# A PEER mixer's second products: weights of four experts per load, first products loaded into the lower parts' buffers, routing recorded between the steps of the weights' making

## Chip, cores and metric

The kernel runs on one core of one Trainium2 chip. The metric is the device time of one execution in microseconds, 3498.06 us before the change (median of three runs, 3488.26 to 3505.14).

## What is computed

A decoder block of 1024 tokens and width 1024: two attention mixers, memory attention, and then a PEER mixer. In the PEER mixer each token has, for each of 8 heads, the 16 best of 128 x 128 experts; an expert is one row of `u` and one row of `v`:

```python
q = (hf @ w_q).reshape(n, PEER_HEADS, 2, PEER_HALF)
sc = einsum('nhcd,hckd->nhck', q, sub_keys)
s_top, i_top = top_k(sc, PEER_TOPK)
...
best_s, pos = top_k(cand_s, PEER_TOPK)
best_i = take_along_axis(cand_i, pos)
g = softmax(best_s)
...
a = einsum('cd,ced->ce', hc, u[ic])
a = gelu(a, approximate=False) * gc
out = einsum('ce,ced->cd', a, v[ic])
```

## The kernel before

Tokens are cut into eight blocks of 128. The attention phases and all products that feed the mixer end about 1629 us after the start of the span; the change leaves their work alone. Blocks 0 to 3 get their mixer by gathers: GpSimd (POOL) fetches 128 rows of `u` (L1035) or of `v` (L1051) by an indirect DMA, and VectorE (DVE) takes a product with them (L1038 for `u`, L1057 for `v`). There are 1024 such gathers, 512 KB each. They are a lane of a pacer (`pace`), which records one of them after each so many microseconds of TensorE work, and run beside everything else, to the end.

Blocks 4 to 7 get theirs in `dense` (L1190), by full products over all 16384 experts in 128 parts of 128; below, "expert" stands for such a part. For each expert there is a first product, `first` (24 matmuls into `acc`: tokens of the four blocks against 128 rows of `u`, L135 to L137), a Gelu, a product with the expert's weights `wl` (L1252, which are zero where a token did not choose it), and a second product with 128 rows of `v`. Every operand is split into two parts that TensorE multiplies at full rate: ACT copies it to the upper part (L112), DVE subtracts to the lower (L113), and three matmuls stand for one. So `uraw` becomes `uT0` and `uT1`, `vraw` becomes `v0` and `v1`, the weighted Gelu becomes `c0` and `c1`.

In time `dense` has these stages.

- Weights stage, 1630 to 2209 us. `weights` (L1116) makes the table of weights for the four blocks as a lane of the pacer, beside the first products of the first 48 experts (`early`), whose Gelu goes to DRAM as `ga` (256 KB each). For each block it first runs the routing (`route`, top 16 and the choice of 16 among the sums, nearly all on DVE, 21 pieces), then two transposes and the codes (L1131 to L1152), then 32 steps: two matmuls to `dot` (L1164), a Relu on ACT (`oh`, L1168), a comparison on DVE (`ah`, L1170), four matmuls to `out` (L1174), a copy on ACT to `wbuf` (L1176). After 16 steps a half of the block is stored to `Wd` by eight stores of 512 KB (L1184) on SP's queue, released one at a time in the pieces of the routing and the steps that follow. What of this lane is left when the 48 first products are recorded is drained without any beside it.
- Start of the second products, 2209 to 2244 us.
- Stage of the loaded first products (the "ga stage" below), 2244 to 2561 us: groups 0 to 10 of second products. A group is four experts: `second` loads their `vraw` (512 KB each, four buffers), splits them and issues 96 matmuls, into four PSUM tiles that are kept over all groups (`kept`) and into two that DVE adds to `accu` (L1281). For the next group, `group` loads the weights of two experts at a time (`wl`, 128x8x128, L1244), and for each expert its stored first product (`c`, one buffer, L1248).
- Steady stage, 2561 to 3478 us: groups 11 to 31, where `group` makes the first products itself, so that a group has 96 first and 96 second matmuls. Then the end, to 3497 us.

SP issues all of these loads in one order, and waits in it: an issue that waits for a buffer holds up all behind it. The order on each engine is set by a scheduler at build time.

## Time and profile before

| | us |
|---|---|
| median of three runs | 3498.06 |
| the profiled execution | 3498.35 |
| its span | 3496.6 |
| TensorE busy (matmul) | 3027.1 |
| DVE busy | 2851.4 |
| ACT busy | 1399.1 |
| POOL busy | 1402.9 |

Busy times are sums over the whole span, and no engine of them is the limit all the way; so the stages are read apart, each with its busy times, the granted clock of TensorE and the share of time that the DMA engines were busy, and then the waits of each engine inside a stage.

### The profile page before, as it was taken

Reading aid. Unit: us, or ns where it says so; the run is one execution under the profiler, and the core shown is the slowest. Engines: PE = TensorE matmul, PEld = TensorE weight load, DVE = VectorE, ACT = ScalarE, POOL = GpSimd, SP = SyncE. Lnnn points to the kernel's source line nnn. Section 1 sums busy time; section 2 is a strip of 40 time slices with the busy share of each in tenths; the row PEclk is TensorE's granted clock in tenths of the full one; section 3 lists DMA queues with packets and bytes.
Section 4 is the critical chain, followed back from the end, with each engine's and each line's share of the span. In section 5 each row is a group of like instructions: output and inputs, shape, how many; then the busy total and the mean of one; then the engine's idle time right before and its main releaser. Section 6 shows DMA issues by size and latency. Waiting matters only on the chain. (4 is left out here: it accounts for less than half of the span.)

```text
span 3496.6 us, 42268 instructions
## 1 busy us (share of the span) xinstructions
PE 3027.1 (87%) x13234; PEld 2292.2 (66%) x13234; DVE 2851.4 (82%) x6623; ACT 1399.1 (40%) x2537; POOL 1402.9 (40%) x1122
## 2 busy tenths in 40 slices
PE   8999888798788798777998896587899999999997
PEld 6778766553345675445676674466677888787886
DVE  6656554588968989887999888687799999899998
ACT  5756344245656441323546465222122222222222
POOL 0010000012245346653122665424457666776665
PEclk9999999899898899888999998799899999999999
DMA  4575443335789579887485999989899999999998
GB/s 139 163 187 136 168 136 137 128 121 187 215 285 303 145 263 359 305 322 281 141 294 210 372 366 345 381 305 326 304 349 373 384 381 371 359 365 384 377 380 285
DMA packets 394210, 964.64 MB, mean 276 GB/s; under 512 B 36713, under 2 KB 146049, under 8 KB 392577
## 3 DMA queue, kind: packets, MB, share of 16 engines
q0 software_dynamic: 155264, 560.01, 45.1%
q1 hardware_dynamic: 238720, 401.94, 33.5%
q8 instruction: 104, 1.70, 0.2%
q14 instruction: 122, 0.99, 0.1%
HBM read 871.64 MB, written 90.18 MB: 275 GB/s over the span
## 5 line engine op out<-in xcount | busy, mean ns | idle before, releaser
L1035 POOL DMA_INDIRECT rows<-in_peer_u_dram,ii x512 | 689.0, 1346 | 916.8 <-DVE rows L1038 365.5
L1051 POOL DMA_INDIRECT rows<-in_peer_v_dram,ii x512 | 649.6, 1269 | 425.4 <-DVE h3s L1057 290.3
L1057 DVE SCALAR_TENSOR_TENSOR h3s<-rows,wexp,h3s 128x1024 f32<-128x1024 f32 x508 | 651.0, 1282 | 36.3 <-DMA rows<-in_peer_v_dram,ii 27.4
L1038 DVE SCALAR_TENSOR_TENSOR rows<-rows,h3s 128x1024 f32<-128x1024 f32 x512 | 611.6, 1219 | 79.1 <-DMA rows<-in_peer_u_dram,ii 75.7
L135 PE MATMUL acc<-fT,uT 128*128 128x512 f32 x1024 | 415.1, 405 | 43.3 <-ACT uT L112 23.9
L137 PE MATMUL acc<-fT,uT 128*128 128x512 f32 x1024 | 412.3, 403 | 13.8 <-DVE uT L113 13.7
L136 PE MATMUL acc<-fT,uT 128*128 128x512 f32 x1024 | 409.6, 400 | 0.0
L112 ACT ACTIVATE c<-wl 128x512 fp32r<-128x512 f32 x128 | 80.1, 631 | 812.2 <-PE out L136 461.6
L149 POOL TENSOR_TENSOR rstd<-msq,mhalf 128x1 f32<-128x1 f32 (+1 forms) x42 | 35.3, 840 | 592.9 <-DVE msq L147 582.5
L135 PEld LDWEIGHTS acc<-fT,uT 128*128 128x128 f32 x1024 | 196.8, 192 | 88.7 <-ACT uT L112 24.8
L137 PEld LDWEIGHTS acc<-fT,uT 128*128 128x128 f32 x1024 | 196.7, 192 | 66.5 <-DVE uT L113 20.9
L136 PE MATMUL kept<-v,c 128*128 128x512 f32 x512 | 206.7, 406 | 34.5 <-DVE v L113 34.5
L135 PE MATMUL kept<-v,c 128*128 128x512 f32 x512 | 202.3, 401 | 37.8 <-ACT v L112 36.9
L112 ACT ACTIVATE uT<-uraw 128x1024 fp32r<-128x1024 f32 x128 | 135.5, 1059 | 246.8 <-PE acc L136 130.5
L136 PEld LDWEIGHTS acc<-fT,uT 128*128 128x128 f32 x1024 | 196.9, 192 | 38.7
L113 DVE TENSOR_TENSOR w<-wraw,w 128x512 fp32r<-128x512 f32 (+1 forms) x176 | 116.8, 680 | 118.6 <-ACT w L112 112.0
L135 PE MATMUL out<-v,c 128*128 128x512 f32 x512 | 204.1, 399 | 8.9 <-DVE accu L1281 8.9
L137 PE MATMUL kept<-v,c 128*128 128x512 f32 x512 | 203.9, 398 | 0.0
L136 PE MATMUL out<-v,c 128*128 128x512 f32 x512 | 202.9, 396 | 0.0
L137 PE MATMUL out<-v,c 128*128 128x512 f32 x512 | 202.6, 396 | 0.0
L568 ACT ACTIVATE junk<-W,xb 128x384 bf16<-128x384 f32 (+5 forms) x186 | 163.7, 880 | 75.7 <-DVE xb L566 55.2
L112 ACT ACTIVATE w<-wraw 128x512 fp32r<-128x512 f32 (+1 forms) x176 | 105.9, 619 | 186.5 <-PE acc L136 81.8
(361 smaller groups left out, 6780.8 us busy)
## 6 DMA issues: line engine op xcount, KB each, us to landing
uraw<-in_peer_ut_dram SPq DMA_DIRECT2D x128, 512.0 KB
vraw<-in_peer_v_dram SPq DMA_DIRECT2D x128, 512.0 KB
Wd<-wbuf SPq DMA_DIRECT2D x64, 512.0 KB
wl<-Wd SPq DMA_DIRECT2D x64, 512.0 KB
wraw<-in_w_in_dram SPq DMA_DIRECT2D x40, 512.0 KB
fraw<-in_w_in_dram SPq DMA_DIRECT2D x32, 512.0 KB
wraw<-in_w_out_dram SPq DMA_DIRECT2D x24, 512.0 KB
ga<-gelu SPq DMA_DIRECT2D x48, 256.0 KB
```

Source lines behind the costliest of these rows:

```text
L112: self.nc.scalar.activation(hi, src, AF.Copy)
L113: self.last_dve = self.nc.vector.tensor_tensor(lo, src, hi.bitcast(F32), op=OP.subtract).ins
L135: nc.tensor.matmul(out, l[0], r[0], start=start, stop=False)
L136: nc.tensor.matmul(out, l[0], r[1], start=False, stop=False)
L137: self.last_pe = nc.tensor.matmul(out, l[1], r[0], start=False, stop=stop).ins
L149: nc.gpsimd.tensor_tensor(r, v, self.mhalf[:, :n], op=OP.pow)
L568: nc.scalar.activation(junk[:, :(b + 1) * P], self.W[b], AF.Sign, bias=xb[:, j:j + 1].bitcast(F32), accum_out=s[:, j:j + 1])
L1035: nc.gpsimd.indirect_dma_start(out=u, out_offset=None, in_=a["peer_u"][0], in_offset=bass.IndirectOffsetOnAxis(ap=ii[:, j:j + 1], axis=0))
L1038: nc.vector.scalar_tensor_tensor(u, u, 1.0, h3, op0=OP.mult, op1=OP.mult, accum_out=aa[:, j:j + 1])
L1051: nc.gpsimd.indirect_dma_start(out=v, out_offset=None, in_=a["peer_v"][0], in_offset=bass.IndirectOffsetOnAxis(ap=r["ii"][:, j:j + 1], axi ...
L1057: nc.vector.scalar_tensor_tensor(o, v, w[:, j:j + 1], o, op0=OP.mult, op1=OP.add)
```

## The change

Four things are changed. The load of weights brings those of four experts, a whole group (128x8x256, 1 MB, in runs of 1 KB), in place of two (512 KB, in runs of 512 bytes), still into two buffers: 32 loads for 64. The stored first product has no tile of its own any more: it is loaded into the expert's `c1`, which has seven buffers, and which the split overwrites later. `vraw` has three buffers for four. In `weights` the routing of block j+1 is recorded in the steps of block j, one piece in each of the first 21 steps, and a piece no longer releases a store. On the side, the Gelu of the gathered rows is made in place (`wexp` goes) and `aa` has two buffers for three. The line numbers of the code behind L1120 are higher by up to four in the kernel after.

```diff
@@ -1029,7 +1029,7 @@
         ii = r["ii"]
         h3 = ep.tile([P, D], F32, name="h3s", bufs=1)
         nc.sync.dma_start(h3, self.h3[b])
-        aa = r["aa"] = ep.tile([P, P], F32, name="aa", bufs=3)
+        aa = r["aa"] = ep.tile([P, P], F32, name="aa", bufs=2)
         for j in range(P):
             u = self.rows()
             nc.gpsimd.indirect_dma_start(out=u, out_offset=None, in_=a["peer_u"][0],
@@ -1041,8 +1041,8 @@
     def gathered_v(self, b, r):
 
         nc, a, ep = self.nc, self.a, self.ep
-        w = ep.tile([P, P], F32, name="wexp", bufs=1)
-        nc.scalar.activation(w, r["aa"], AF.Gelu)
+        w = r["aa"]
+        nc.scalar.activation(w, w, AF.Gelu)
         nc.vector.tensor_tensor(w, w, r["gg"], op=OP.mult)
         o = ep.tile([P, D], F32, name="h3s", bufs=1)
         for j in range(P):
@@ -1121,12 +1121,12 @@
         wb = self.wb
         self.make_codes()
         stores = []
+
+        r = {}
+        yield from self.route(blks[0], r)
         for j, b in enumerate(blks):
-            r = {}
-            for us in self.route(b, r):
-                if stores:
-                    stores.pop(0)()
-                yield us
+            rn = {}
+            ahead = self.route(blks[j + 1], rn) if j + 1 < len(blks) else iter(())
             t = self.ps.tile([P, 512], F32, name="out", bufs=2)
             nc.tensor.transpose(t[:, :P], r["ids"].rearrange("p h s -> p (h s)"), self.ident)
             nc.tensor.transpose(t[:, P:2 * P], r["g"].rearrange("p h s -> p (h s)"), self.ident)
@@ -1176,13 +1176,15 @@
                 nc.scalar.activation(wbuf[:, :, m:m + 4].rearrange("p e n -> p n e"), o, AF.Copy)
                 if stores:
                     stores.pop(0)()
-                yield 1.0
+                yield 1.0 + next(ahead, 0.0)
                 if m + 4 == H:
                     for e0 in range(0, P, 16):
                         def store(e0=e0, at=2 * j + n0 // H, wbuf=wbuf):
                             with self.tc.issue_after(self.last_load):
                                 nc.sync.dma_start(self.Wd[at, :, e0:e0 + 16], wbuf[:, e0:e0 + 16])
                         stores.append(store)
+            yield from ahead
+            r = rn
         while stores:
             stores.pop(0)()
             yield 3.0
@@ -1239,18 +1241,19 @@
             def group(gi):
                 cs = []
                 for e in range(gi * G, gi * G + G):
-                    if e % 2 == 0:
-                        w2 = sp.tile([P, 2 * ND, 2, P // 2], F32, name="wl", bufs=2)
-                        nc.sync.dma_start(w2, self.Wd[:, :, e:e + 2].rearrange("j p e n -> p j e n"))
-                    w = w2[:, :, e % 2]
+                    if e % G == 0:
+                        wg = sp.tile([P, 2 * ND, G, P // 2], F32, name="wl", bufs=2)
+                        nc.sync.dma_start(wg, self.Wd[:, :, e:e + G].rearrange("j p e n -> p j e n"))
+                    w = wg[:, :, e % G]
+                    ch = [sp.tile([P, DT], F32R, name=f"c{j}", bufs=7) for j in range(2)]
                     if e in ga:
-                        c = sp.tile([P, DT], F32, name="c", bufs=1)
+
+                        c = ch[1].bitcast(F32)
                         nc.sync.dma_start(c, ga[e])
                     else:
                         c = first(e)
                         nc.scalar.activation(c, c, AF.Gelu)
                     nc.vector.tensor_tensor(w, c.rearrange("p (j n) -> p j n", j=2 * ND), w, op=OP.mult)
-                    ch = [sp.tile([P, DT], F32R, name=f"c{j}", bufs=7) for j in range(2)]
                     self.split(w, *[x.rearrange("p (j n) -> p j n", j=2 * ND) for x in ch])
                     cs.append(ch)
                 return cs
@@ -1391,7 +1394,7 @@
 WHOLE = {("P", 1), ("G", 1), ("M", 1)}
 PAIRS = {(2, 0)}
 KEEP, A_BUFS, O_BUFS = 4, 2, 2
-U_BUFS, V_BUFS = 3, (4, 4, 4)
+U_BUFS, V_BUFS = 3, (4, 4, 3)
 SELECT_EACH = (5.0, 7.0)
 U_EACH, ROUTE_EACH = (1.9, 1.8, 1.9, 1.3, 2.0), 3.0
 ROUTE_LAG, EXPERT_LAG = 300, 3000
```

Three places show what this moves. The first is SP's queue at the start of the second products; a name like `c_18903<-ga_13694` is the load of one stored first product. Before:

```order
L1244 DMA wl<-Wd 128x8x128 [waits DMAHW2_49,PE_49]
L1248 DMA c<-ga_13695 128x512 [waits DMAHW3_49]
L1244 DMA wl<-Wd 128x8x128 [waits DMAHW4_49]
L1263 DMA vraw<-in_peer_v_dram 128x1024 [waits DMAHW5_49,PE_49]
L1263 DMA vraw<-in_peer_v_dram 128x1024 [waits DMAHW6_49]
L1248 DMA c<-ga_13780 128x512 [waits DMAHW7_49,DMAHW3_49,DVE_49]
L1263 DMA vraw<-in_peer_v_dram 128x1024 [waits DMAHW0_49]
L1263 DMA vraw<-in_peer_v_dram 128x1024 [waits DMAHW1_49,Pool_49]
L1248 DMA c<-ga_13853 128x512 [waits DMAHW7_49,DMAHW2_49,DVE_49]
L1263 DMA vraw<-in_peer_v_dram 128x1024 [waits DMAHW5_49,Activation_49]
```

And with the change:

```order
L1246 DMA wl<-Wd 128x8x256 [waits DMAHW2_49,PE_49]
L1252 DMA c_18903<-ga_13694 128x512 [waits DMAHW3_49]
L1252 DMA c_18909<-ga_13779 128x512 [waits DMAHW6_49,DMAHW7_49,DMAHW5_49,DMAHW4_49]
L1252 DMA c_18915<-ga_13852 128x512
L1252 DMA c_18921<-ga_13953 128x512
L1246 DMA wl<-Wd 128x8x256
L1252 DMA c_18929<-ga_14054 128x512 [waits DMAHW0_49]
L1252 DMA c_18935<-ga_14112 128x512 [waits DMAHW1_49]
L1252 DMA c_18941<-ga_14165 128x512 [waits DMAHW2_49]
L1266 DMA vraw<-in_peer_v_dram 128x1024 [waits DMAHW3_49]
L1266 DMA vraw<-in_peer_v_dram 128x1024 [waits DMAHW4_49]
L1266 DMA vraw<-in_peer_v_dram 128x1024 [waits DMAHW5_49]
```

Seven loads of first products and two of weights stand ahead of the first `vraw`, for one and two before; the names read `c_...` although the tile is `c1`.

The second is DVE at the boundary of two groups in the ga stage (`v1` is the lower part of an expert's `v`, the rows L1252 or L1256 the product of a stored first product with its weights, L1281 or L1284 the addition to `accu`, L1038 a gather's product). Before:

```order
L113 TENSOR_TENSOR c1_20316<-wl_20303,c0_20315 128x512
L113 TENSOR_TENSOR v1_20510<-vraw_20511,v0_20509 128x1024
L1281 TENSOR_TENSOR accu_18901<-accu_18901,out_20460 128x512
L113 TENSOR_TENSOR c1_20483<-wl_20477,c0_20482 128x512
L113 TENSOR_TENSOR c1_20490<-wl_20477,c0_20489 128x512
L113 TENSOR_TENSOR v1_20516<-vraw_20517,v0_20515 128x1024
L1252 TENSOR_TENSOR wl_20493<-c_20495,wl_20493 128x8x64
L113 TENSOR_TENSOR v1_20522<-vraw_20523,v0_20521 128x1024
L113 TENSOR_TENSOR c1_20499<-wl_20493,c0_20498 128x512
L113 TENSOR_TENSOR v1_20528<-vraw_20529,v0_20527 128x1024
L1252 TENSOR_TENSOR wl_20493<-c_20502,wl_20493 128x8x64
```

And with the change:

```order
L113 TENSOR_TENSOR v1_20448<-vraw_20449,v0_20447 128x1024
L1256 TENSOR_TENSOR wl_20237<-c1_20258,wl_20237 128x8x64
L1284 TENSOR_TENSOR accu_18899<-accu_18899,out_20404 128x512
L1256 TENSOR_TENSOR wl_20421<-c1_20424,wl_20421 128x8x64
L113 TENSOR_TENSOR c1_20258<-wl_20237,c0_20257 128x512
L1256 TENSOR_TENSOR wl_20421<-c1_20430,wl_20421 128x8x64
L113 TENSOR_TENSOR c1_20424<-wl_20421,c0_20423 128x512
L1256 TENSOR_TENSOR wl_20421<-c1_20436,wl_20421 128x8x64
L113 TENSOR_TENSOR c1_20430<-wl_20421,c0_20429 128x512
L113 TENSOR_TENSOR v1_20454<-vraw_20455,v0_20453 128x1024
L113 TENSOR_TENSOR c1_20436<-wl_20421,c0_20435 128x512
L113 TENSOR_TENSOR v1_20460<-vraw_20461,v0_20459 128x1024
```

Between the first and the second `v1` of a group stand four products with loaded first products, for none before (there one stands between the second and the third). On SP the four loads that these products need stand together, and wait for TensorE; without the change each waits for DVE alone:

```order
L1252 DMA c_19516<-ga_15418 128x512 [waits DMAHW2_49,PE_49]
L1252 DMA c_19685<-ga_15549 128x512 [waits PE_49]
L1252 DMA c_19691<-ga_15653 128x512 [waits DMAHW4_49,PE_49]
L1252 DMA c_19697<-ga_15761 128x512 [waits DMAHW5_49,PE_49]
L1266 DMA vraw<-in_peer_v_dram 128x1024 [waits DMAHW6_49,DVE_49]
L1266 DMA vraw<-in_peer_v_dram 128x1024 [waits DMAHW7_49,DVE_49]
L1246 DMA wl<-Wd 128x8x256 [waits DMAHW0_49,DVE_49]
```

The third is TensorE behind the last matmul of the 48 early first products. Before:

```order
L136 MATMUL acc<-fT_12994,uT_18248 128x512
L137 MATMUL acc<-fT_12993,uT_18249 128x512
L1131 MATMUL out<-ident,ids 128x128
L1132 MATMUL out<-ident,gw 128x128
L1151 MATMUL out<-ident,bi 112x128 x8
L1164 LDWEIGHTS code_18387
L1164 MATMUL dot<-codes,code_18387 128x512
L1151 MATMUL out<-ident,bi 112x128 x8
L1164 LDWEIGHTS code_18409
```

And with the change:

```order
L136 MATMUL acc<-fT_12993,uT_18124 128x512
L137 MATMUL acc<-fT_12992,uT_18125 128x512
L1164 LDWEIGHTS code_17101
L1164 MATMUL dot<-codes,code_17101 128x512
L1164 LDWEIGHTS code_17123
L1164 MATMUL dot<-codes,code_17123 128x512
L1164 LDWEIGHTS code_17101
L1164 MATMUL dot<-codes,code_17101 128x512
L1164 LDWEIGHTS code_17123
L1164 MATMUL dot<-codes,code_17123 128x512
L1174 MATMUL out<-ah,oh 128x128 x3
```

Before, the transposes and codes of the last block come next, and then its 32 steps. With the change it is the steps of the block before the last: 45 steps are left without first products beside them.

## Rows read from the trace of the kernel before

**Rows 1.** the page, busy time of each engine over the span.

```profile
PE 3027.1 (87%) x13234; PEld 2292.2 (66%) x13234; DVE 2851.4 (82%) x6623; ACT 1399.1 (40%) x2537; POOL 1402.9 (40%) x1122
```

**Rows 2.** five stages: stretch, length, busy us of each engine, granted clock, DMA share, GB/s.

```profile
1630.00:2209.00 579.00, 493.61 (x2551) 386.34 (x2552) 510.32 (x1535) 308.01 (x390) 224.13 (x180) 0.94 0.79 288
2209.00:2244.00 35.00, 0.90 (x4) 0.48 (x3) 15.49 (x15) 3.64 (x5) 11.06 (x11) 0.57 1.04 399
2244.00:2561.00 317.00, 269.80 (x1054) 211.85 (x1054) 249.49 (x343) 72.92 (x98) 122.72 (x96) 0.90 0.91 313
2561.00:3478.00 917.00, 895.11 (x3892) 734.06 (x3890) 870.32 (x1049) 252.15 (x330) 614.07 (x446) 0.99 1.00 371
3478.00:3497.00 19.00, 0.07 (x1) 0.00 (x0) 13.16 (x15) 3.45 (x6) 3.44 (x3) 0.55 0.46 170
```

**Rows 3.** the same for two stretches late in the weights stage.

```profile
2110.00:2140.00 30.00, 10.55 (x40) 7.71 (x41) 21.57 (x34) 7.95 (x12) 15.12 (x11) 0.54 0.94 351
...
2170.00:2200.00 30.00, 22.61 (x147) 17.90 (x145) 27.65 (x31) 24.59 (x30) 20.24 (x16) 1.00 1.02 408
```

**Rows 4.** DVE's waits, 1629 to 2216 us: total us, times, longest us.

```profile
DVE rows L1038 <- DMA rows<-in_peer_u_dram,ii: 21.4, 14, 4.9
...
DVE v L935 <- DMA so<-pq: 5.5, 3, 3.2
```

**Rows 5.** TensorE's waits in the same window.

```profile
PE out L1151 <- DVE bi L1146: 31.9, 6, 17.4
```

**Rows 6.** timeline of SP's queue from 2195 us: start, length, instruction.

```profile
2216.88 1.35 SPq L1244 DMA_DIRECT2D wl<-Wd  x1
2218.28 4.82 SPq L1248 DMA_DIRECT2D c<-ga  x1
2223.15 1.73 SPq L1244 DMA_DIRECT2D wl<-Wd  x1
2224.98 11.06 SPq L1263 DMA_DIRECT2D vraw<-in_peer_v_dram  x2
```

**Rows 7.** timeline around the first second product; in brackets the idle time ahead.

```profile
2239.43 0.69 DVE L1252 TENSOR_TENSOR wl<-c,wl 128x512 f32<-128x512 f32 x1 [10.06 <-DMA c<-ga]
...
2243.64 0.79 PE L135 MATMUL kept<-v,c 128*128 128x512 f32 x1 [34.10 <-ACT v L112]
```

**Rows 8.** DVE's waits, 2244 to 2561 us.

```profile
DVE wl L1252 <- DMA c<-ga: 33.3, 24, 2.9
DVE wl L1252 <- DMA wl<-Wd: 17.9, 5, 5.0
DVE wl L1252 <- issue: 6.8, 2, 3.6
```

**Rows 9.** TensorE's waits, 2209 to 2561 us.

```profile
PE kept L135 <- ACT v L112: 36.9, 2, 34.1
PE kept L136 <- DVE v L113: 34.5, 18, 4.7
```

**Rows 10.** DVE's lines, 2244 to 2561 us: busy us, mean ns of one, idle before.

```profile
L113 DVE TENSOR_TENSOR v<-vraw,v 128x1024 fp32r<-128x1024 f32 x44 | 53.1, 1218 | 0.5 <-ACT v L112 0.5
L1057 DVE SCALAR_TENSOR_TENSOR h3s<-rows,wexp,h3s 128x1024 f32<-128x1024 f32 x32 | 41.0, 1280 | 0.2
L1252 DVE TENSOR_TENSOR wl<-c,wl 128x512 f32<-128x512 f32 x47 | 32.5, 691 | 58.2 <-DMA c<-ga 33.3 <-DMA wl<-Wd 17.9 <-issue 6.8
...
L1281 DVE TENSOR_TENSOR accu<-accu,out 128x512 f32<-128x512 f32 x39 | 26.6, 682 | 6.5 <-PE out L137 6.4
```

**Rows 11.** timeline of SP's queue in the ga stage.

```profile
2424.58 0.32 SPq L1248 DMA_DIRECT2D c<-ga  x1
```

**Rows 12.** timeline of DVE in the ga stage.

```profile
2428.81 0.69 DVE L1252 TENSOR_TENSOR wl<-c,wl 128x512 f32<-128x512 f32 x1 [1.38 <-DMA c<-ga]
```

**Rows 13.** a stretch of 100 us in the steady stage.

```profile
2760.00:2860.00 100.00, 100.00 (x443) 82.80 (x442) 98.97 (x95) 25.30 (x33) 67.74 (x52) 1.00 1.01 379
```

**Rows 14.** TensorE's waits, 2561 to 3478 us.

```profile
PE acc L135 <- DVE wl L1252: 19.3, 10, 4.8
```

## Prediction, made before the kernel with the change was run

> **What bounds the kernel now.** I read the busy times of the whole span first [rows 1]: TensorE 87%, DVE 82%. No engine is full throughout, so one limit can't be named for all of it. I read the stages next [rows 2], and there three cases are to be seen. In the weights stage DVE works 510.32 of 579 us and TensorE 493.61: DVE is nearer to its limit. In the ga stage, 317 us, TensorE works 269.80, DVE 249.49, and the DMA engines have a share of 0.91: nobody is full, so it is waits that decide. In the steady stage TensorE works 895.11 of 917, DVE 870.32, DMA 1.00: everything is full. Between the first two lie 35 us in which TensorE does nearly nothing. What the change can return is therefore at most the idle time of TensorE in each stage: 85, 34, 47 and 22 us.
>
> Then the waits. In the ga stage TensorE waits for the lower part of `v` from DVE, 34.5 us in 18 waits, and 34.1 us once at the start [rows 9]. DVE in turn waits for the loaded first product (33.3 us), for the weights (17.9) and for an issue (6.8) [rows 8], all of them waits of one instruction, the product with the weights: 58.0 us in all. As DVE runs in order, the split of `v` behind that product is late by as much.
>
> **The size of a group in the ga stage.** In a full stretch TensorE retires 443 matmuls in 100 us [rows 13], 0.226 us each, so the 96 of a group take 21.7 us. The stage holds 11 groups in 317 us, 28.8 each: 7.1 us of each group are lost. DVE's own work is 249.49 / 11 = 22.7 us per group.
>
> **Part 1, routing between the steps.** Nothing is removed; the same DVE work stands elsewhere. Two things come to it. The wait for the scores, 5.5 us [rows 4], goes, since there is other work on DVE now while they are loaded. And six more gathers fall into this stage (185 before, 191 now, counted in the order of DVE): 6 x 1.28 [rows 10] = +7.7. The end of the stage runs without first products for 45 steps, not 32. That costs nothing as long as DVE is as full there as elsewhere: in the last full stretch it works 27.65 of 30 us [rows 3], since gathers fill it; without that cover, 13 steps more would be paid at the pace of the end, where 32 of them fill the 69 us from 2140 to 2209, 2.1 us each: +27. Against that stands one stretch that shows what the routing costs as it is: from 2110 to 2140 TensorE works 10.55 us at a granted clock of 0.54, near the lower of its two levels, 1.2 GHz [rows 3], and a long wait there is that of the transposes for the codes' bits, 17.4 of 31.9 us [rows 5]. If DVE were not the limit, the 19.5 idle us of that stretch would be the gain, -20. As DVE is the limit, I take the sum of the two certain pieces, **+2** (-20 to +27).
>
> **Part 2, the start.** Ahead of the first `vraw` SP now issues two loads of weights of 1 MB and seven first products, against two of 0.5 MB and one [rows 6]: 1.05 + 6 x 0.262 = 2.6 MB more. At the 399 GB/s of these 35 us [rows 2] that is 6.6 us by which the first `v` comes later. Before, the first product with loaded data ends an idle time of 10.06 us, and the first matmul starts at 2243.64, behind the split of `v` [rows 7]; so it moves by the full amount. **+6.5**. The lower bound is 0, if the `v` loads move past the others in the DMA engines; the upper one +16, if the seven products and splits that now stand ahead of the split of `v` on DVE (14 x 0.69 [rows 10] = 9.7) are not hidden by its load.
>
> **Part 3, ga stage.** One buffer for the loaded first product means one load at a time: issued at 2424.58 [rows 11], its product starts at 2428.81 [rows 12], after 4.2 us, and only then can the next be issued. That chain is gone, and so is the wait for weights: a whole group's load is issued one group ahead. But the change puts another wait in its place. `c1` comes free when TensorE finishes a group, so four loads of first products are issued together at that moment, T, and on DVE their four products stand between the first and second `v1` of the group that TensorE is starting. Worked out: first load at T + 4.2. Then come, row by row in the order of DVE: product, addition to `accu`, product, split, product, split, product, split, each 0.69 [rows 10], and the second `v1`, 1.22: 8 x 0.69 + 1.22 = 6.7 us. So the second `v1` is ready at T + 10.9. TensorE has 23 matmuls ahead of the first that needs it (counted in its order), 23 x 0.226 = 5.2 us, and waits 5.7. The third and fourth `v1` follow at T + 12.8 and T + 14.0, about when TensorE comes to them. A group takes 21.7 + 5.7 = 27.4, 1.4 less than before; ten groups, **-14**. Two more gathers in the stage (90, now 92) give back 2 x 1.28: **-11.5** (-50 to +28, the rivals below). Behind the four loads on SP stands the fourth `vraw`, which now waits for a buffer too (three for four): its split is due at T + 14, 9 us after it can be issued, more than the 4.2 us of a load, so I cost it at nothing; without that cover it would cost the same 1 or 2 us in each group.
>
> **Part 4, steady stage.** Eight gathers fewer (456, now 448): 8 x 1.28 = 10 us of DVE. But TensorE is idle for only 22 us there, 19.3 of them waiting for the product with the weights [rows 14], so I count half, **-5** (-20, all its idle time, to +20, 1 us for each of 20 groups if `vraw` with three buffers makes a `v1` late). The fewer and longer runs of the `wl` loads I count at nothing, since no wait of TensorE there names a DMA.
>
> A bound for that last piece: the ga stage moves 313 GB/s at a share of 0.91, the steady one 371 at 1.00 [rows 2]. At the latter's rate per share, the 99.2 MB of the ga stage would need 267 us of full DMA, and they took 0.91 x 317 = 288: 21 us of DMA time are the most that better-formed loads could return there. The Trainium skill, "DMA: Bandwidth & Descriptors", section Specifications, gives 512 bytes as the smallest transfer at line rate; by that rule, going from 512 bytes to 1 KB would return 0, and the sum stays. The rows do not tell the share of `wl` in the 21 us.
>
> **Sum.** 2 + 6.5 - 11.5 - 5 = -8. The profiled execution took 3498.35, 0.3 above the median of the runs: 3490.35, said as **3490 us**. That is 0.2%, inside the 0.5% (17.5 us) which is about what a measurement of this kernel can tell from no change.
>
> **Rival A, faster.** DVE reaches the four products late anyway, because gathers' products and additions fill it, and finds the loads landed: its 58 us of waits go. Then the stage falls to the next limit, which is DMA, 267 us at the steady rate. That is -50 in place of -11.5: 3498 + 2 + 6.5 - 50 - 5 = **3452**. For it: DVE has 22.7 us of work per group, more than TensorE's 21.7. Against it: the order shows no gather's product between the first and the second `v1`.
>
> **Rival B, slower.** The four loads don't land at 0.8 us from each other but behind what is under way. In the start, where the DMA share is 1.04, the first such load was issued at 2218.28 [rows 6] and used at 2239.43 [rows 7]. If a group's worth stands ahead of the four, four gathers and two `vraw`, 3 MB, and if 2 of the 4.2 us of a single load are not its transfer, the fourth lands at T + 2 + 4.2 MB / 399 GB/s = T + 12.5. Behind it come product, split and `v1`, 2.6 us: T + 15.1, a wait of 9.9, a group of 31.6, +28 over ten groups. It decides from the point where a group takes the 28.8 of before: `v1` at T + 12.3, fourth load at **T + 9.7**. With +16 for the start: 3498 + 2 + 16 + 28 + 2.5 - 5 = **3542**. For it: DMA at 0.91 in the stage, and every gather in the queue is 512 KB. Against it: loads issued one at a time take 4.2 us in the same stage.
>
> **Chances.** Forecast (the waits change places, within 0.5%) 0.40. Rival A or a good part of it 0.35: two of the three causes of DVE's waits do go, and only the timing of the third is in doubt. Rival B or a late `vraw` 0.25. The forecast's own range is the sum and 17.5 us to either side, 3473 to 3508. The whole range goes to A and to B, 3452 to 3542, which leaves one in ten on either side for what lies beyond their worked prices. Faster 0.35, same 0.40, slower 0.25.
>
> **What would show it.** In the profile after: DVE's wait for the loaded first product in the ga stage between 20 and 45 us, and none for `wl`; SP's wait before that load on TensorE instead of DVE; TensorE's wait for the lower part of `v` about 5 us, once in each group; the first second product some 6 us later behind the last `Wd` store than before; the weights stage within 20 us of 579, its route gap at half clock gone but a longer tail. It is wrong if the ga stage ends under 285 us or over 335, if the weights stage moves by more than 20, or if the steady stage, with nothing idle to give, moves by more than 20.

## The result, and the profile after

The changed kernel takes 3597.88 us, median of four runs (3593.84 to 3612.29); the kernel before, on the same chip, 3500.11. The ratio is 1.030, with a 95% interval of 1.027 to 1.032: about 100 us slower, beyond the range that was given.

The profiled execution has a span of 3598.7 us, 102.1 more than before. Its stages, in the form of [rows 2] (the limits are this kernel's own: the first store of the last eight, the first second product, the end of group 10, the last second product):

```profile
1630.00:2182.00 552.00, 480.11 (x2512) 374.23 (x2513) 507.40 (x1534) 312.77 (x388) 224.37 (x179) 0.96 0.81 299
2182.00:2234.00 52.00, 9.45 (x42) 7.51 (x40) 30.06 (x31) 8.19 (x12) 17.61 (x17) 0.62 1.02 393
2234.00:2547.00 313.00, 266.60 (x1057) 207.64 (x1058) 248.44 (x343) 72.65 (x93) 132.13 (x99) 0.93 0.90 311
2547.00:3574.00 1027.00, 931.07 (x3887) 753.32 (x3887) 860.80 (x1032) 249.64 (x330) 600.29 (x439) 0.94 0.91 326
```

| us | before | after | difference |
|---|---|---|---|
| first of the last eight stores of the weights | 2199.8 | 2181.7 | -18.1 |
| from there to the first second product | 43.8 | 52.5 | +8.7 |
| ga stage (groups 0 to 10) | 317.9 | 312.6 | -5.3 |
| steady stage (groups 11 to 31) | 916.1 | 1027.2 | +111.1 |
| from the last second product to the end | 18.9 | 24.6 | +5.7 |

So the whole loss, and more, lies in the stage that I had at -5. TensorE does the same matmuls there, but its busy time grows from 895 to 931 us and its idle time by 74. Its waits in that stage (engine, line, what it waited for: total us, times, longest):

```profile
PE acc L135 <- DVE wl L1256: 94.0, 22, 10.1
...
PE kept L135 <- ACT v L112: 0.7, 1, 0.7
```

The wait for the product with the weights was 19.3 us before [rows 14] and is 94.0. DVE, which makes that product, has waits that it did not have before, and so has ACT. Before, DVE waited longest for gathered rows in this stage, and the only load that ACT waited for was that of `uraw`:

```profile
DVE rows L1038 <- DMA rows<-in_peer_u_dram,ii: 32.5, 23, 5.8
```

```profile
ACT uT L112 <- DMA uraw<-in_peer_ut_dram: 6.9, 4, 2.7
```

With the change, DVE's first:

```profile
DVE v L113 <- ACT v L112: 87.9, 15, 10.2
DVE c L113 <- ACT c L112: 47.0, 7, 9.1
```

ACT's waits in the same stage:

```profile
ACT v L112 <- DMA vraw<-in_peer_v_dram: 163.8, 21, 15.3
```

The timelines of one group show how one becomes the other: SP's queue first (start, length, instruction; in brackets the idle time ahead), then ACT, DVE and TensorE.

```profile
2889.14 0.38 SPq L1246 DMA_DIRECT2D wl<-Wd  x1
2892.07 2.60 SPq L1266 DMA_DIRECT2D vraw<-in_peer_v_dram  x3
2898.62 0.33 SPq L1205 DMA_DIRECT2D uraw<-in_peer_ut_dram  x1
2906.11 0.33 SPq L1266 DMA_DIRECT2D vraw<-in_peer_v_dram  x1
```

```profile
2887.02 2.94 ACT L112 ACTIVATE v<-vraw 128x1024 fp32r<-128x1024 f32 x3
...
2894.98 0.58 ACT L1255 ACTIVATE acc<-acc 128x512 f32<-128x512 f32 x1
2902.61 1.06 ACT L112 ACTIVATE v<-vraw 128x1024 fp32r<-128x1024 f32 x1 [7.05 <-DMA vraw<-in_peer_v_dram]
2903.57 0.61 ACT L112 ACTIVATE c<-wl 128x512 fp32r<-128x512 f32 x1
```

```profile
2890.82 3.49 DVE L113 TENSOR_TENSOR v<-vraw,v 128x1024 fp32r<-128x1024 f32 x3
...
2897.35 1.21 DVE L113 TENSOR_TENSOR uT<-uraw,uT 128x1024 fp32r<-128x1024 f32 x1
2904.22 0.69 DVE L113 TENSOR_TENSOR c<-wl,c 128x512 fp32r<-128x512 f32 x1 [5.66 <-ACT c L112]
...
2908.30 0.68 DVE L1256 TENSOR_TENSOR wl<-acc,wl 128x512 f32<-128x512 f32 x1
```

```profile
2909.04 0.79 PE L135 MATMUL acc<-fT,uT 128*128 128x512 f32 x1 [4.00 <-DVE wl L1256]
```

A, B and C, the first three `vraw` of the group, have been loaded early and are split at 2887 to 2894. D, the fourth, needs A's buffer, which DVE's split sets free at 2892; SP issues D and the next two at 2892.07. The split of D, which waits for its landing, starts 10.5 us later, at 2902.61; ACT has been idle for 7.05 us by then. On ACT that split stands ahead of the upper part `c0` of the next group's first expert, so `c0` is held up with it, and behind `c0` the split of `uT` and the next Gelu (L1255, 2905.04). So is DVE's `c1`, which has DVE idle for 5.66 us; then the product with the weights that would free an `acc` buffer, and TensorE 4.00 us. D itself is not needed so soon: the second products of its group start at 2917.04, and TensorE waits for no `v` there. Over the stage the landing of a `vraw` takes 11.4 us (the row has the number of loads, the size and the time from issue to landing, a median of those loads whose landing the trace shows, fewer than half of the 81):

```profile
vraw<-in_peer_v_dram SPq DMA_DIRECT2D x81, 512.0 KB, 11.4
```

### The profile page after: what moved, and what is told of

Same layout as the page of the kernel before. It is cut to its first block, busy times and chain, and to the rows that moved or that the text cites. A ratio compares the mean times of both kernels' runs of the same rounds, so it can differ in the third digit from the quotient of the medians.

```text
span 3598.7 us, 42141 instructions
## 1 busy us (share of the span) xinstructions
PE 3051.9 (85%) x13234; PEld 2301.1 (64%) x13234; DVE 2853.3 (79%) x6623; ACT 1405.3 (39%) x2537; POOL 1403.3 (39%) x1122
## 4 chain that ended last, share of the span: by engine, by line
PE 32%; DVE 23%; DMA 16%; issue 16%; POOL 7%; ACT 4%; SPq 1%; POOLq 0%; ACTq 0%; DVEq 0%
DMA vraw<-in_peer_v_dram 5%; PE acc L135 4%; PE acc L137 4%; PE acc L136 4%; POOL rows L1035 4%; DVE rows L1038 3%; DVE h3s L1057 3%; POOL rows L1051 3%; DMA rows<-in_peer_u_dram,ii 2%; DMA rows<-in_peer_v_dram,ii 2%; DMA so<-pq 2%; PE po L727 2%; PE kept L136 1%; DMA fraw<-in_w_in_dram 1%; PE kept L137 1%
## 5 line engine op out<-in xcount | busy, mean ns | idle before, releaser
L1057 DVE SCALAR_TENSOR_TENSOR h3s<-rows,aa,h3s 128x1024 f32<-128x1024 f32 x508 | 650.9, 1281 | 30.5 <-DMA rows<-in_peer_v_dram,ii 21.1
L1038 DVE SCALAR_TENSOR_TENSOR rows<-rows,h3s 128x1024 f32<-128x1024 f32 x512 | 609.3, 1218 | 59.1 <-DMA rows<-in_peer_u_dram,ii 58.4
L135 PE MATMUL acc<-fT,uT 128*128 128x512 f32 x1024 | 432.5, 422 | 114.3 <-DVE wl L1256 94.0
L137 PE MATMUL acc<-fT,uT 128*128 128x512 f32 x1024 | 421.6, 412 | 4.8 <-DVE uT L113 4.6
L136 PE MATMUL acc<-fT,uT 128*128 128x512 f32 x1024 | 421.9, 412 | 0.0
L135 PEld LDWEIGHTS acc<-fT,uT 128*128 128x128 f32 x1024 | 203.5, 199 | 167.0 <-DVE wl L1256 103.5
L112 ACT ACTIVATE c<-wl 128x512 fp32r<-128x512 f32 x128 | 80.0, 628 | 556.3 <-PE out L136 303.5
L149 POOL TENSOR_TENSOR rstd<-msq,mhalf 128x1 f32<-128x1 f32 (+1 forms) x42 | 34.1, 812 | 598.3 <-DVE msq L147 580.8
L112 ACT ACTIVATE v<-vraw 128x1024 fp32r<-128x1024 f32 x128 | 128.2, 1049 | 338.1 <-DMA vraw<-in_peer_v_dram 192.6
L137 PEld LDWEIGHTS acc<-fT,uT 128*128 128x128 f32 x1024 | 202.4, 198 | 69.0 <-DVE uT L113 15.3
L136 PEld LDWEIGHTS acc<-fT,uT 128*128 128x128 f32 x1024 | 204.4, 200 | 41.5 <-issue 0.8
L136 PE MATMUL kept<-v,c 128*128 128x512 f32 x512 | 206.1, 403 | 29.0 <-DVE v L113 28.8
L113 DVE TENSOR_TENSOR v<-vraw,v 128x1024 fp32r<-128x1024 f32 x128 | 152.4, 1218 | 93.6 <-ACT v L112 93.6
L135 PE MATMUL out<-v,c 128*128 128x512 f32 x512 | 203.2, 397 | 16.4 <-DVE accu L1284 16.4
## 6 DMA issues: line engine op xcount, KB each, us to landing
wl<-Wd SPq DMA_DIRECT2D x32, 1024.0 KB, 12.1
```

Source lines behind the costliest of these rows:

```text
L112: self.nc.scalar.activation(hi, src, AF.Copy)
L113: self.last_dve = self.nc.vector.tensor_tensor(lo, src, hi.bitcast(F32), op=OP.subtract).ins
L135: nc.tensor.matmul(out, l[0], r[0], start=start, stop=False)
L136: nc.tensor.matmul(out, l[0], r[1], start=False, stop=False)
L137: self.last_pe = nc.tensor.matmul(out, l[1], r[0], start=False, stop=stop).ins
L149: nc.gpsimd.tensor_tensor(r, v, self.mhalf[:, :n], op=OP.pow)
```

## Experiments

Twelve kernels. Stage limits are those of the table above.

| kernel | stores begin | to first product | ga stage | steady | end | median us | ratio to before, 95% interval |
|---|---|---|---|---|---|---|---|
| before | 2199.8 | 43.8 | 317.9 | 916.1 | 18.9 | | |
| changed | 2181.7 | 52.5 | 312.6 | 1027.2 | 24.6 | 3597.88 | 1.030 (1.027 to 1.032) |
| e1_vraw3 | 2205.6 | 43.9 | 336.2 | 1002.4 | 25.7 | 3612.42 | 1.032 (1.028 to 1.035) |
| e8_vlate | 2186.9 | 52.5 | 307.3 | 923.9 | 27.4 | 3500.75 | 1.001 (0.998 to 1.003) |
| e14_vlate_dve | 2186.5 | 52.2 | 318.0 | 1014.6 | 25.8 | 3597.16 | 1.029 (1.027 to 1.032) |
| e2_after_vraw4 | 2181.4 | 51.6 | 303.5 | 918.9 | 19.5 | 3475.89 | 0.995 (0.993 to 0.997) |
| e3_route | 2178.1 | 43.7 | 330.1 | 912.3 | 18.9 | 3484.82 | 0.996 (0.993 to 0.999) |
| e4_ga | 2196.4 | 48.1 | 328.4 | 917.8 | 18.9 | 3510.97 | 1.005 (1.003 to 1.006) |
| e6_route_ga | 2184.2 | 48.4 | 317.0 | 917.2 | 19.3 | 3489.40 | 0.998 (0.996 to 1.000) |
| e9_start | 2182.6 | 46.3 | 316.6 | 917.5 | 38.9 | 3503.64 | 1.003 (1.002 to 1.005) |
| e10_vlate_start | 2179.7 | 46.6 | 315.2 | 930.8 | 24.3 | 3505.03 | 1.002 (1.000 to 1.004) |
| e11_best_start | 2186.0 | 47.0 | 300.5 | 932.8 | 25.1 | 3493.31 | 1.001 (0.999 to 1.002) |
| e12_best_wl2 | 2179.0 | 48.0 | 343.5 | 909.9 | 19.7 | 3503.28 | 1.003 (1.001 to 1.004) |
| e15_runs512 | 2178.4 | 53.0 | 302.0 | 935.9 | 19.5 | 3491.28 | 0.999 (0.997 to 1.000) |

The stages are of one execution each.

### Three buffers for vraw alone

```diff
-U_BUFS, V_BUFS = 3, (4, 4, 4)
+U_BUFS, V_BUFS = 3, (4, 4, 3)
```

> The kernel before with one edit: three buffers for vraw instead of four. Theory 1 (the fourth vraw of a group is issued only when a buffer is split free at the end of a group, and its split, first in line on ACT and DVE, holds up the next group's first products): the steady stage grows from 917 by about the 116 us that it grew with the whole change, total 3500 + 116 = 3616, 3590 to 3630. Theory 2 (the 1 MB loads of weights and the bursts of four loads are what slows the steady stage, not the buffers): within 20 us of 3500.

3612 us, as theory 1 had it. The one edit, with loads of two experts' weights and everything else as before, makes the steady stage 86 us longer (about 116 had been expected) and the ga stage 18. The waits of ACT in the steady stage are those of the changed kernel (163.8 us in 21 waits there):

```profile
ACT v L112 <- DMA vraw<-in_peer_v_dram: 163.9, 20, 16.2
```

So large loads of weights and bursts of four are not needed for the loss.

### The changed kernel with the split of D queued later

```diff
+                    if e not in ga:
+                        marks[e] = self.last_act, self.last_dve
                     cs.append(ch)
...
-                    self.split(raw, vv[0], vv[1])
+                    m = marks.get((gi + 1) * G + 1) if e % G == G - 1 else None
+                    with ExitStack() as late:
+                        for i in m or ():
+                            late.enter_context(self.tc.issue_after(i))
+                        self.split(raw, vv[0], vv[1])
```

> The changed kernel with one edit: in the steady stage the split of the fourth vraw is queued on ACT and DVE behind the split of the next group's second product (c0, c1 of its second expert) instead of ahead of the first one. Three buffers stay. Theory 1: the load may land late without harm, only the order of the engines does the harm; the steady stage falls from 1033 to 920 to 960 us, total 3490 to 3525. Theory 2 (transfers themselves too slow, or vraw needed when it lands): no change, 3580 to 3600.

The steady stage falls from 1027 to 924 us, the whole by 97 to 3500.75, with three buffers and landings that are as late (median 12.2 us). Of ACT's wait for `vraw` 14.6 us remain, of TensorE's for the product 21.7. ACT's waits in the steady stage of this kernel:

```profile
ACT v L112 <- DMA vraw<-in_peer_v_dram: 14.6, 8, 4.3
```

and TensorE's:

```profile
PE acc L135 <- DVE wl L1258: 21.7, 13, 3.9
```

The load is late, but what costs is where the instruction that waits for it stands.

### Later on DVE alone

```diff
-                        for i in m or ():
+                        for i in m[1:] if m else ():
```

(against the kernel above)

> The changed kernel with the split of the fourth vraw queued later on DVE alone; on ACT it stays ahead of the next group's first c0. If ACT's order does the harm (c0 stands behind a v0 that waits for its load, and everything after it needs c0 or the Gelu behind it): nothing or little comes back, 3570 to 3600. If it is DVE's order: 3500 to 3520, as with both moved.

Nothing comes back, 3597 us: moving the split on DVE alone does not help, and it has to move on ACT. (ACT alone was not tried.) DVE's wait for `v` has gone (87.9 us in the changed kernel), and a wait for `c0` is in its place, since that is still behind D on ACT. The waits of ACT, of DVE and of TensorE in this kernel's steady stage:

```profile
ACT v L112 <- DMA vraw<-in_peer_v_dram: 164.1, 21, 12.3
```

```profile
DVE c L113 <- ACT c L112: 123.4, 20, 8.9
...
DVE v L113 <- ACT v L112: 3.8, 2, 3.5
```

```profile
PE acc L135 <- DVE wl L1258: 85.8, 21, 8.2
```

The Trainium skill, "Perfetto Trace Analysis", section "Tensor Engine Instruction (MATMUL, LD_WEIGHTS)", calls ACT and DVE strict first-in first-out; by that rule a split that is not ready holds up all behind it, and the changed kernel, this one and the one above agree, with 94, 86 and 22 us of waits on TensorE.

### The changed kernel with four buffers

```diff
-U_BUFS, V_BUFS = 3, (4, 4, 3)
+U_BUFS, V_BUFS = 3, (4, 4, 4)
...
-                    ch = [sp.tile([P, DT], F32R, name=f"c{j}", bufs=7) for j in range(2)]
+                    ch = [sp.tile([P, DT], F32R, name=f"c{j}", bufs=6 + j) for j in range(2)]
```

> The changed kernel with four buffers of vraw again; to make room, the upper part c0 has six buffers instead of seven. Theory 1 (the third buffer is the whole loss): steady stage within 15 us of 917, ga stage 295 to 305 instead of 313 (three buffers alone added 18 us there in the kernel before), total 3470 to 3490. If the six buffers of c0 cost something themselves, or the large loads of weights do: over 3500.

3475.89 us, 0.995 of before (0.993 to 0.997), the fastest of the study: 122 less than the changed kernel. The steady stage is 918.9, and ACT has no wait for `vraw` in it. With four buffers of `vraw` (and six of `c0`) the rest of the change is a gain of about 20 us.

### Routing between the steps, alone

```diff
+        yield from self.route(blks[0], r)
         for j, b in enumerate(blks):
-            r = {}
-            for us in self.route(b, r):
...
+            rn = {}
+            ahead = self.route(blks[j + 1], rn) if j + 1 < len(blks) else iter(())
...
-                yield 1.0
+                yield 1.0 + next(ahead, 0.0)
```

> The kernel before with the routing of block j+1 recorded in the steps of block j, nothing else. If the last store of the weights comes 18 us earlier for this part, as it does with the whole change (first of the last eight at 2181.72 for 2199.80): total 3500 - 18 = 3482, 3475 to 3490. If DVE is the limit of the stage, as the prediction had it: 3500, within 8 us, and the 18 us come from another part.

The last stores begin 21.7 us sooner, and the first second product 21.8; it is this part that shortens the weights stage. In all kernels with it the last stores begin at 2178 to 2187 us, in the three without it at 2196 to 2206. The ga stage gives 12.2 back, though none of its code is changed; why was not looked into. Differences of that size between two ga stages of one run each can't be put down to an edit. TensorE's wait for the codes' bits, 31.9 us before [rows 5], is 13.9 in the weights stage of this kernel and 12.1 in that of the changed one (TensorE's waits, in this order):

```profile
PE out L1151 <- DVE bi L1146: 13.9, 4, 5.4
```

```profile
PE out L1151 <- DVE bi L1146: 12.1, 4, 5.1
```

### First products into c1, alone

```diff
-                        c = sp.tile([P, DT], F32, name="c", bufs=1)
+                        c = ch[1].bitcast(F32)
```

> The kernel before with the stored first products loaded into c1, nothing else. By the prediction's terms: start later by the six more loads ahead of vraw, 6 x 0.262 MB at 399 GB/s = +4, ga stage -11.5: total 3492. By what the two kernels with the routing moved differ in (start +10.7, ga stage -13.1, steady stage +4.9): total 3500 within 8 us. If the bursts of four loads harm: ga stage longer than 318.

3510.97 us, 0.5% slower. That is neither of the two totals that had been worked out. The start is 4.3 us later, about the 3.9 us that the bytes ahead of `vraw` come to; the ga stage is 10.5 longer, not 11.5 shorter. With the routing moved as well (e6_route_ga) the expectation was

> The kernel before with the routing between the steps and the stored first products loaded into c1, but weights of two experts per load and four buffers of vraw. Theory 1: the steady stage is that of before, 917 within 10; weights stage -18, start +0 to +7, ga stage -4 to -15: total 3470 to 3490. Theory 2 with the bursts of four loads as the cause: ga stage longer than 317, total over 3500.

and 3489.40 was measured, with the ga stage at 317.0 and the steady stage at 917.2. The same edit thus comes with a ga stage 10.5 us longer than that of the kernel before, and 13.1 shorter than that of the kernel with the routing alone (330.1): neither a gain nor a harm of the bursts in that stage is shown.

### Loads of weights: of two experts, or in runs of 512 bytes

Both kernels are that with four `vraw` and six `c0` (3476 us). The first loads two experts' weights at a time, into two tiles of two; the second fills the tile of four by two loads of two:

```diff
-                        nc.sync.dma_start(wg, self.Wd[:, :, e:e + G].rearrange("j p e n -> p j e n"))
+                        for h in range(0, G, 2):
+                            nc.sync.dma_start(wg[:, :, h:h + 2], self.Wd[:, :, e + h:e + h + 2].rearrange("j p e n -> p j e n"))
```

> The kernel of the fourth vraw buffer and six c0 (3476 us), but with weights of two experts per load (512 KB, runs of 512 bytes). If the larger loads of weights are what makes its ga stage 13.5 us shorter than with weights of two experts and seven c0 (303.5 for 317.0): 3476 + 13 = 3489. If it is the six c0 or chance: 3476.

> The fastest kernel (four vraw, six c0, 3476 us), with the same 1 MB tile of weights for four experts but filled by two loads of two experts each, in runs of 512 bytes. If what the larger load of weights brings (ga stage 303.5 against 343.5 us) is that a group's weights are under way a group ahead (two tiles of four experts): no change, 3476, and DVE's wait for wl stays near 2 us. If it is the length of the runs: ga stage towards 340, total 3490 to 3505.

With tiles of two experts the ga stage takes 343.5 us for 303.5, 40 more, where 13.5 had been expected (with seven `c0` and tiles of two, in e6_route_ga, it took 317.0, with 95 gathers' products in it; whether the six cost something there was not followed up); with the tile of four in runs of 512 bytes it takes 302.0. Some of the 40 are work that another stage is spared: the longer ga stage holds 111 gathers' products for 102, 12 us of DVE, and its steady stage is 9.0 us shorter. In the whole kernel 27 us are left (3503.28 for 3475.89). DVE's waits for `wl` in the ga stage are these, first with tiles of two (read from 2234 to 2560 us), then with tiles of four in long runs, then with tiles of four in short runs:

```profile
DVE wl L1256 <- DMA wl<-Wd: 19.5, 9, 5.2
```

```profile
DVE wl L1256 <- DMA wl<-Wd: 2.3, 1, 2.3
```

```profile
DVE wl L1257 <- DMA wl<-Wd: 1.2, 1, 1.2
```

So in the ga stage, with six `c0`, it is the tile that is filled a group ahead which counts, not the length of its runs. The total does not say so: with short runs it is 3491.28, 12 us below that with tiles of two and 15 above that with long runs, as its steady stage is the longest of the three. That TensorE waits 64.0 us for the lower part of `v` with tiles of two and 32.0 with tiles of four says where the 40 us show (TensorE's waits in the ga stage, in this order):

```profile
PE kept L136 <- DVE v L113: 64.0, 17, 10.2
```

```profile
PE kept L136 <- DVE v L113: 32.0, 9, 6.6
```

In the steady stage the kernel with short runs is 17 us slower (935.9 for 918.9). The queue that carries the loads moves as many bytes there in a larger share of the time (short runs first, then long ones: packets, MB, share of the 16 DMA engines' time in the stage):

```profile
q1 hardware_dynamic: 63003, 105.20, 31.3%
```

```profile
q1 hardware_dynamic: 43274, 105.32, 30.6%
```

31.3% of 936.1 us is 293, 30.6% of 919.0 is 281: 12 us more. (It is 294 and 291 in e12_best_wl2 and e6_route_ga, which have short runs too, and 280 and 279 in e8_vlate and e11_best_start, which have long ones.) By the rule of the Trainium skill, "DMA: Bandwidth & Descriptors", section Specifications, that runs of 512 bytes reach line rate, there would be nothing; here the DMA engines' time is against it. Whether the stage is longer for it is another matter: e11_best_start, with long runs, has 932.8 us in the steady stage as well (there with 442 gathers' products in it, where these two have 432 and 433), and the six kernels that load tiles of two in runs of 512 bytes and have four `vraw` (the one before, e3_route, e4_ga, e6_route_ga, e9_start, e12_best_wl2) have 910 to 918. How much of the 17 us is the runs' stays open.

### Sooner at the start

```diff
-                nx = group(gi + 1) if gi + 1 < NE // G else None
-                second(gi, cs)
+                vs = loads(gi) if gi == 0 else None
+                nx = group(gi + 1) if gi + 1 < NE // G else None
+                second(gi, cs, vs or loads(gi))
```

(`loads` is the first half of `second`, with the loads and splits of `vraw`.) It was tried on three kernels.

> Routing between the steps, stored first products into c1, weights of two experts, four buffers of vraw, and the first group's vraw loads recorded ahead of the second group's loads, so that four stored first products stand ahead of the first vraw instead of seven. If the queue ahead of vraw sets the start: three loads fewer, 0.8 MB at 399 GB/s = 2 us, up to the 10.7 us by which the start is later with c1 than with a tile of its own; ga stage 317 as without this edit: total 3489 - 2 to 3489 - 11. If DVE's seven products set the start: no change, 3489.

> The changed kernel with the split of the fourth vraw queued later and with the first group's vraw loads recorded ahead of the second group's. If the queue ahead of vraw sets the start, which here holds 2.5 MB more than before (of them 1.8 MB go with this edit, 4.6 us at 399 GB/s): 3501 - 4.6 to 3501 - 10, so 3490 to 3496. Otherwise 3501.

> The kernel of the fourth vraw buffer and six c0 (3476 us) with the first group's vraw loads recorded ahead of the second group's loads. The first second product comes 2 to 6 us sooner (46.4 us behind the first of the last eight stores instead of 51.6, as in the two other kernels with this edit). If the rest of the stages follows: 3470 to 3474. If, as with weights of two experts, gathers are left over at the end: 3476 to 3495.

The first second product comes 2.1, 5.9 and 4.6 us sooner behind the stores. That the queue ahead of `vraw` sets the start is not shown by it, since the edit moves two things forward: the loads, and their splits on ACT, which had stood behind the next group's `c0`. Without the edit the first split of `vraw` waits 1.93 us for its load on the first kernel, not at all on the second (it follows the seventh `c0`) and 0.65 on the third. But none of the three is faster than the kernel that it was tried on (3503.64 for 3489.40, 3505.03 for 3500.75, 3493.31 for 3475.89): the end is 20 us longer in the first, the ga and the steady stage 8 and 7 in the second, the steady stage and the end 14 and 6 in the third. In the first, 14 products of gathers are left for after the last second product, where five are in the kernel that it was tried on, and in the fastest one (DVE's lines from there to the end, first this kernel, then the fastest: busy us, mean ns, idle):

```profile
L1057 DVE SCALAR_TENSOR_TENSOR h3s<-rows,wexp,h3s 128x1024 f32<-128x1024 f32 x14 | 18.0, 1282 | 1.4 <-DMA rows<-in_peer_v_dram,ii 1.2
```

```profile
L1057 DVE SCALAR_TENSOR_TENSOR h3s<-rows,aa,h3s 128x1024 f32<-128x1024 f32 x5 | 6.4, 1281 | 0.0
```

## Why the prediction was wrong

**The step that failed** is in part 4 (and its twin at the end of part 3): "1 us for each of 20 groups if `vraw` with three buffers makes a `v1` late". It priced the wrong thing. I asked whether TensorE would get its `v1` late, found it would not, which is right (TensorE's only wait for a `v` in the stage is 0.7 us), and took 4.2 us for the landing, which is that of a load of half the size in the ga stage. A `vraw` in the steady stage lands 11.4 us after its issue, and the price is paid by those who stand behind its split on ACT: the next group's first products, 111 us in the stage, some 5.3 for each of 21 groups, where the upper bound had 1. The order of ACT, where the fourth `v0` stands ahead of the first `c0`, could be read before the run; I did not read it. With e1_vraw3 and e2_after_vraw4 on either side, and e8_vlate with the buffer still missing and only the order changed, this is shown. (Alone, in the kernel before, the missing buffer costs the steady stage 86 us; that it costs 111 with the rest of the change was not followed up.) The sign of being wrong that the prediction named, a steady stage that moves by more than 20, is the one that came.

**Part 1**, +2 predicted, -18.1 measured (-21.7 alone). The mechanism at the lower bound was right, and the reason against it wrong: "as DVE is the limit". DVE was idle for 69 of 579 us, and 24 of these went with the routing's blocks (it works 507.40 of 552 us in the profile after). What ended TensorE's stall of 17.4 us was not more DVE time, but the routing being done by the time its result was wanted. The longer end without first products did come: from the last of the early first products to the last of the steps it is 103 us now (2074.9 to 2177.5) for 88 before (2107.7 to 2195.6). But those products, with 13 steps fewer beside them, are through 33 us sooner, and that the sum did not have.

**Part 2**, +6.5 predicted, +8.7 measured: the number is near, its reason was another. The first second product is at 2234.24, 42.8 us of waiting for `v` ahead of it, where 34.1 were [rows 7, 9]. Before, the first split of `v` on ACT had waited for its load:

```profile
2242.53 2.10 ACT L112 ACTIVATE v<-vraw 128x1024 fp32r<-128x1024 f32 x2 [1.75 <-DMA vraw<-in_peer_v_dram]
```

With the change it does not wait for its load. It stands behind seven `c0`, and the last of them waits for DVE (DVE's first product of the start, then ACT):

```profile
2224.30 1.89 DVE L1256 TENSOR_TENSOR wl<-c,wl 128x512 f32<-128x512 f32 x3 [10.79 <-DMA c<-ga]
```

```profile
2232.61 0.63 ACT L112 ACTIVATE c<-wl 128x512 fp32r<-128x512 f32 x1 [0.74 <-DVE wl L1256]
2233.15 2.97 ACT L112 ACTIVATE v<-vraw 128x1024 fp32r<-128x1024 f32 x3
```

DVE's first product comes 42.6 us behind the first of the last stores, 3.0 more than before; from there to the first second product it is 9.9 us, for 4.2. So two thirds of the 8.7 are the seven products and splits, which the prediction had for its upper bound alone, and on DVE. That the two came out alike is luck.

**Part 3**, -11.5 predicted, -5.3 measured, -14.4 with the fourth buffer back. The boundary went as worked out. In group 3 the four loads are issued at 2312.83, and on DVE:

```profile
2314.14 1.22 DVE L113 TENSOR_TENSOR v<-vraw,v 128x1024 fp32r<-128x1024 f32 x1
2317.10 0.69 DVE L1256 TENSOR_TENSOR wl<-c,wl 128x512 f32<-128x512 f32 x1 [1.75 <-DMA c<-ga]
...
2321.92 1.21 DVE L113 TENSOR_TENSOR v<-vraw,v 128x1024 fp32r<-128x1024 f32 x1
```

4.3 us to the first product (4.2 assumed), the second `v1` done 10.3 us after the issue (10.9 assumed). DVE waits 33.0 us for first products, inside the 20 to 45 that were given, and SP's wait is on TensorE. TensorE's waits did not go as worked out: for `v1` it waits 28.8 us in 15 waits, 4.0 at most, where 5.7 in each of ten groups had been reckoned, and 16.4 us in nine waits for additions to `accu`, which the sum did not have (8.9 in three before); its idle time in the stage is 46 us as it was 47. A `vraw` makes ACT wait there as well, 28.8 us in ten waits. What the sum had wrong is the cause: landing in `c1` is not shown to bring anything by itself (e4_ga +10.5, e6_route_ga -13.1, which is how such stages scatter), while e12_best_wl2 and e15_runs512 show a gain in this stage from the weights being loaded a group ahead. With differences of 12 us between stages of equal code, the 14.4 are not clear of scatter as they stand.

**Part 4**, the rest, -5 predicted, +111.1 measured: DVE's eight gathers fewer were counted for a gain that could not be seen beside the loss.

**The rivals.** A did not come (312.6 us, not 267). B's end was right by accident: slower, but its place was the ga stage, and in group 3 the fourth load did not land at T + 9.7 or later, since its product starts at T + 7.9 (2320.72) with no wait. What came, ACT held up by a late buffer, was not among them; a late `vraw` stands there as half a sentence, with a price of 20 us and another mechanism.

## What to carry to other kernels

When a pool loses a buffer, the load that now waits is the one to follow: when it can be issued, how long a load takes to land in that stage (not in a quieter one), and which instruction waits for it. What then counts is not whether its data are late for their use, but what is queued behind that instruction on its engine; either the buffer stays, or the waiting instruction is moved behind work that is ready. A load that is issued a group ahead needs a tile for a whole group ahead; in the ga stage, with six `c0`, that was worth 40 us (27 in the whole kernel), and the length of the load's runs nothing.

## What was not expected of the hardware

TensorE's clock takes a third of the loss. In the steady stage its busy time is 36.7 us longer for the same matmuls (894.6 to 931.3), its waits 74.1 (21.7 to 95.8): together 110.8 of the 111.1. The granted clock of the stage falls from 0.99 [rows 2] to 0.94; in the timeline the first matmul behind the wait of 4.00 us takes 0.79 us, as a matmul at the lower of the two levels (1.2 GHz) does at the start of the second products [rows 7]. From 2909.0 to 2913.9 the granted clock is 0.50, and the 12 matmuls behind the wait take 5.2 us from start to start, for 2.7 at the pace of those that follow: 2.5 us more in this group, on top of the wait. The prediction took TensorE's idle time for all that a stage can move by; busy time moves with the clock. In e8_vlate, with the wait for the product back at 21.7 us, the clock is back at 0.99:

```profile
2546.00:3470.00 924.00, 898.51 (x3889) 735.11 (x3888) 861.68 (x1035) 252.97 (x330) 593.85 (x439) 0.99 0.97 363
```

(A stretch of 924 us, with the columns of [rows 2]: TensorE's busy time is 898.51.)
